# FFN input projections of a hybrid decoder trunk: Strassen's seven quarter products for eight, with the tokens on the partitions

## The chip, the cores and the metric

One core of a Trainium2 chip. The metric is the device time of one execution of the whole program, in microseconds. Activations and weights are float32 and lie in DRAM at the start; weights are laid out ahead of time by the host (copies and reorderings alone, no arithmetic).

## The reference, cut to what matters

Two layers, each a token mixer (retention in layer 0, a gated linear recurrence in layer 1) and a SwiGLU feed-forward network (FFN), each behind and ahead of an RMS norm. S = 512 tokens, D = 1024 features, FFN width 2816.

```
def rms_norm(x, g):
    y = xf * lax.rsqrt(jnp.mean(xf * xf, axis=-1, keepdims=True) + NORM_EPS)
    return y * g

def swiglu_ffn(x, w_in, w_out):
    gate, up = jnp.split(x @ w_in, 2, axis=-1)
    return (jax.nn.silu(gate) * up) @ w_out

for layer in range(2):
    m = mixer(rms_norm(x, norm_g[layer, 0]))
    x = x + rms_norm(m, norm_g[layer, 1])
    f = swiglu_ffn(rms_norm(x, norm_g[layer, 2]), ffn_w_in[layer], ffn_w_out[layer])
    x = x + rms_norm(f, norm_g[layer, 3])
```

`x @ w_in` is the FFN input projection: 512 x 1024 times 1024 x 5632.

## The kernel before

Activations are held with the features on the 128 partitions and the 512 tokens along the row. Every float32 product is made as three products of a shortened float32 format (fp32r): an operand is split into a high part (a cast) and a low part (value minus high part), and high·high, high·low and low·high are added up in PSUM (`mm3`, L189 to L191). Weights arrive as raw chunks of 128x1024, loaded by SP's queue; ACT makes the high part (L145, `wh_...`), DVE the low part (L146, `wl_...`). Four raw chunks are loaded ahead and up to eight are held split.

The order of the program is written by a recording scheme: PE's products are issued one after another, and work of the other engines is put off by so many ns of products (`Later`); each engine then works through its own list in order.

Between two matrix products stands a norm. `out_proj` ends with `finish`, which for each half of the tokens takes 1/rms of the projection (`rchain`: a matmul sums the squares, `st_...`, DVE makes the root by a short chain, a matmul broadcasts it, `rb_...` L289), and then goes through the eight feature tiles: DVE multiplies (L358), POOL adds the residual (L362), ACT makes the high part of the next operand (L308, `Xf_0h` and so on) and the squares, POOL adds these up (L326), DVE makes the low part (L312). The FFN's input projection begins on these tiles while they are still being made: `first_groups` runs the first three groups (a group is 128 gate and 128 up columns) side by side, tile by tile, for the first half of the tokens, then for the second. The other 19 groups run one after another, with all 512 tokens. 1/rms of the FFN's own input is applied to the result (`done`: DVE multiplies gate and up by the broadcast `rb_f`, L623 and L624, ACT takes silu, L626, DVE multiplies, L627, and the product is split for the output projection). The two first passes of the value projection (`pv`) have it the other way round: there tokens are the stationary operand of PE, weights the moving one.

Of the kernel before, what the change touches and what calls it, by code (L numbers as in the profile page):

```python
# [88 lines left out]
def trunk(ctx: ExitStack, tc: tile.TileContext, t: dict):  # L89
# [36 lines left out]
    def load():  # L126
        j = st["raw"]
        nm, src, cols, _ = order[j]
        raws[j] = wp.tile([P, 1024], F32, tag="raw", name=f"wr_{nm}", bufs=WRAW)
        nc.sync.dma_start(raws[j][:, :cols], src)  # L130
        st["raw"] += 1

    def load_ahead():
        while st["raw"] < min(st["split"] + WRAW, len(order)):
            load()

    def split_next():
# [4 lines left out]
        raw = raws.pop(j)
        hi = wp.tile([P, 1024], F32R, tag="whi", name=f"wh_{nm}")
        lo = wp.tile([P, 1024], F32R, tag="wlo", name=f"wl_{nm}")
        act.copy(hi[:, :cols], raw[:, :cols])  # L145
# [697 lines left out]
```

## Time and profile before

| | |
|---|---|
| time, median of 3 runs | 1411.14 us (1411.08 to 1411.99) |
| span of the profiled execution | 1409.6 us |
| PE busy | 1383.7 us (98%) |
| DVE busy | 751.4 us (53%) |
| ACT busy | 535.4 us (38%) |
| POOL busy | 115.5 us (8%) |

The span is from the first to the last instruction of the one profiled execution; the times of the runs are some 1.5 us longer. Busy time of an engine is that in which it worked on at least one instruction; a busy PE is not a PE at its peak.

### The profile page before, as it was taken

The numbers are of one execution on the slowest core, as the hardware profiler recorded it, in microseconds if no ns is written. First come the engines' busy times: TensorE is split into PE (matmuls) and PEld (weight loads), VectorE is DVE, ScalarE is ACT, GpSimd is POOL, SyncE is SP. The second block draws the span as 40 slices with busy tenths as digits, with TensorE's granted clock in tenths as the row PEclk, the third lists the DMA queues.
The fourth block names the chain that finished last, engine by engine and source line by source line (L and its number), as shares of the span: only waits on it lengthen the run. The fifth ranks groups of instructions, "written<-read, shape, count | busy, mean of one in ns | idle before, by whom it ended". The sixth has DMA issues, their size and how long they took to land.

```text
span 1409.6 us, 17882 instructions
## 1 busy us (share of the span) xinstructions
PE 1383.7 (98%) x7128; PEld 1188.4 (84%) x7128; DVE 751.4 (53%) x1234; ACT 535.4 (38%) x793; POOL 115.5 (8%) x157
## 2 busy tenths in 40 slices
PE   8999999999999999999999999999999999999996
PEld 6888888888898888888889998888998888888886
DVE  7655455457247545444321787888486444443223
ACT  4423333335234323232222537787454222222320
POOL 1000000001015000000000610001070000000002
PEclk9999999999999999999999999999999999999998
DMA  7223232223324223322342423234342332223322
GB/s 266 90 79 94 71 103 86 76 90 120 120 77 131 94 90 101 109 90 83 128 141 91 141 83 98 90 105 137 108 146 91 94 113 92 90 82 128 104 68 68
DMA packets 49172, 146.81 MB, mean 104 GB/s; under 512 B 5728, under 2 KB 14048, under 8 KB 49088
## 3 DMA queue, kind: packets, MB, share of 16 engines
q1 hardware_dynamic: 45072, 135.16, 29.7%
q0 software_dynamic: 2864, 9.46, 2.3%
q8 instruction: 56, 0.92, 0.3%
q10 hardware_dynamic: 1152, 1.05, 0.2%
q14 instruction: 28, 0.23, 0.1%
HBM read 137.25 MB, written 8.39 MB: 103 GB/s over the span
## 4 chain that ended last, share of the span: by engine, by line
PE 66%; issue 25%; POOL 4%; DVE 2%; ACT 1%; DMA 1%; SPq 0%; POOLq 0%; DVEq 0%
PE ps_fi L190 5%; PE ps_fi L189 5%; PE ps_fi L191 5%; PE ps_fo L189 3%; PE ps_fo L191 3%; PE ps_fo L190 3%; PE ps_g L189 2%; PE ps_g L190 2%; PE ps_g L191 2%; PE ps_ro L189 2%; PE ps_ro L191 2%; PE ps_ro L190 2%; PE pv L189 2%; PE pv L191 2%; PE pv L190 2%
## 5 line engine op out<-in xcount | busy, mean ns | idle before, releaser
L146 DVE TENSOR_TENSOR wl_fi<-wr_fi,wh_fi 128x1024 fp32r<-128x1024 f32 x88 | 110.5, 1260 | 11.1 <-ACT wh_fi L145 11.1
L626 ACT ACTIVATE gr<-gr 128x512 f32<-128x512 f32 x44 | 27.8, 632 | 219.7 <-DVE gr L623 219.7
L623 DVE TENSOR_TENSOR gr<-ps_fi,rb_f 128x512 f32<-128x512 f32 x44 | 30.4, 691 | 132.8 <-PE ps_fi L191 132.8
L145 ACT CAST wh_fi<-wr_fi 128x1024 fp32r<-128x1024 f32 x88 | 91.2, 1043 | 0.0
L624 DVE TENSOR_TENSOR ur<-ps_fi,rb_f 128x512 f32<-128x512 f32 x44 | 30.4, 691 | 82.9 <-PE ps_fi L191 72.5
L146 DVE TENSOR_TENSOR wl_fo<-wr_fo,wh_fo 128x1024 fp32r<-128x1024 f32 (+1 forms) x48 | 52.9, 1132 | 33.5 <-ACT wh_fo L145 33.5
L145 ACT CAST wh_fo<-wr_fo 128x1024 fp32r<-128x1024 f32 (+1 forms) x48 | 45.0, 979 | 30.1 <-DMA wr_fo<-in_w_fo 19.4
L146 DVE TENSOR_TENSOR wl_g<-wr_g,wh_g 128x1024 fp32r<-128x1024 f32 x16 | 19.5, 1222 | 35.0 <-ACT wh_g L145 34.9
L190 PE MATMUL ps_fi<-Xf_0l,wh_fi 128*128 128x512 f32 (+1 forms) x100 | 36.5, 365 | 1.5 <-DVE Xf_0l L312 1.5
L191 PE MATMUL ps_fi<-Xf_4h,wl_fi 128*128 128x512 f32 (+1 forms) x100 | 36.5, 365 | 1.1 <-DVE wl_fi L146 1.1
L189 PE MATMUL ps_fi<-Xf_7h,wh_fi 128*128 128x512 f32 (+1 forms) x100 | 36.6, 366 | 0.6 <-ACT Xf_7h L308 0.6
L189 PE MATMUL ps_fi<-Xf_4h,wh_fi 128*128 128x512 f32 (+1 forms) x100 | 36.5, 365 | 0.4 <-ACT wh_fi L145 0.4
L190 PE MATMUL ps_fi<-Xf_7l,wh_fi 128*128 128x512 f32 (+1 forms) x100 | 36.6, 366 | 0.3
L189 PE MATMUL ps_fi<-Xf_0h,wh_fi 128*128 128x512 f32 (+1 forms) x100 | 36.6, 366 | 0.2 <-ACT ylo L352 0.2
L189 PE MATMUL ps_fi<-Xf_1h,wh_fi 128*128 128x512 f32 (+1 forms) x100 | 36.7, 367 | 0.0
L189 PE MATMUL ps_fi<-Xf_3h,wh_fi 128*128 128x512 f32 (+1 forms) x100 | 36.7, 367 | 0.0
L189 PE MATMUL ps_fi<-Xf_5h,wh_fi 128*128 128x512 f32 (+1 forms) x100 | 36.5, 365 | 0.0
L189 PE MATMUL ps_fi<-Xf_6h,wh_fi 128*128 128x512 f32 (+1 forms) x100 | 36.5, 365 | 0.0
L190 PE MATMUL ps_fi<-Xf_3l,wh_fi 128*128 128x512 f32 (+1 forms) x100 | 36.5, 365 | 0.0
L190 PE MATMUL ps_fi<-Xf_6l,wh_fi 128*128 128x512 f32 (+1 forms) x100 | 36.5, 365 | 0.0
L191 PE MATMUL ps_fi<-Xf_5h,wl_fi 128*128 128x512 f32 (+1 forms) x100 | 36.4, 364 | 0.0
L191 PE MATMUL ps_fi<-Xf_3h,wl_fi 128*128 128x512 f32 (+1 forms) x100 | 36.4, 364 | 0.0
(1375 smaller groups left out, 4420.7 us busy)
## 6 DMA issues: line engine op xcount, KB each, us to landing
wr_fi<-in_w_fi SPq DMA_DIRECT2D x88, 512.0 KB, 4.1
wr_fo<-in_w_fo SPq DMA_DIRECT2D x40, 512.0 KB, 4.4
wr_g<-in_w_g SPq DMA_DIRECT2D x16, 512.0 KB, 5.4
wr_ro<-in_w_ro SPq DMA_DIRECT2D x16, 512.0 KB, 3.8
wr_v<-in_w_v SPq DMA_DIRECT2D x13, 512.0 KB, 3.8
wr_u<-in_w_li SPq DMA_DIRECT2D x12, 512.0 KB, 3.9
wr_y<-in_w_li SPq DMA_DIRECT2D x12, 512.0 KB, 3.7
wr_lo<-in_w_lo SPq DMA_DIRECT2D x12, 512.0 KB, 3.6
```

Of the source, the lines that this page charges most:

```text
L145: act.copy(hi[:, :cols], raw[:, :cols])
L146: dve.tensor_tensor(lo[:, :cols], raw[:, :cols], hi[:, :cols].bitcast(F32), op=ALU.subtract)
L189: pe.matmul(out, lhsT=lh, rhs=rh, start=first, stop=False)
L190: pe.matmul(out, lhsT=lh, rhs=rl, start=False, stop=False)
L191: pe.matmul(out, lhsT=ll, rhs=rh, start=False, stop=last)
L623: dve.tensor_tensor(gr, ps[0], pre.rb, op=ALU.mult)
L624: dve.tensor_tensor(ur, ps[1], pre.rb, op=ALU.mult)
L626: 700, lambda: act.activation(gr, gr, AF.Silu),
```

## The change

Five sixths and more of the FFN's columns (2560 of 2816 gate and as many up columns) are taken in five pairs of 512. For one pair the tokens are cut in two halves, the 1024 inner features in two (even and odd tiles of 128), and the gate and the up columns are the two halves of the columns; the product of two by two quarters is made by Strassen's scheme in Winograd's form, with seven quarter products p1 to p7 in place of eight. Their operands are the quarters themselves and four sums each: s1 to s4 of the tokens' quarters (`Corners`), t1 to t4 of the weights' quarters (`Form`), all made in float32 by DVE and then split in high and low parts as before. Each quarter product is 24 matmuls of 128x512, with tokens as the stationary and weights as the moving operand, so results have tokens on the partitions. They are added up in three pairs of PSUM banks (A, B, C), partly by running on in the same bank, partly by ACT and DVE copies; p1 is put into B by a copy. 1/rms is then a column by partitions and goes in as the scale of silu and as the scalar of a DVE operation; its broadcast falls away. The finished result is turned back by PE (`turn`: four transposes of 128x128 in fp32, one ACT copy), and split in tiles of 1024 (`halve`). The first 256 gate and up columns are made without the scheme. In the opening, the plain columns, p1 and p2 of the first pair run side by side, tile by tile, for the first token half; then the plain columns for the second half, then p6, p5, p7, p3. The last p4 stands inside the output projection.

All big buffers come from one pool of 50 slots of 4 KB, where there were two (58 of 2 KB, and 20 for weights). Residual tiles are loaded two at a time, and two memsets a block go in the recurrence.

The diff, cut to its core:

```diff
+    class Form(Item):
+        SUMS = {"t1": ("b11", "b12"), "t2": ("t1", "b22"), "t3": ("b12", "b22"), "t4": ("t2", "b21")}
+        BEFORE = {"b11": ["t1"], "t1": ["t2"], "b21": ["t4"], "b22": ["t2", "t3"], "t2": ["t4"]}
...
+        def value(self, f):
...
+                dve.tensor_tensor(q[f, e], x, y, op=ALU.add)
...
+    class Corners:
+        SUMS = (("s1", (1, 0), (1, 1), ALU.subtract), ("s2", "s1", (0, 0), ALU.subtract),
+                ("s4", (0, 1), "s2", ALU.add), ("s3", (0, 0), (1, 0), ALU.subtract))
...
+            add(*by["s1"])
+            add(*by["s2"])
+            later.seq(lambda: None, 2500, lambda: two("s2"), 2500, lambda: two("s1"), W_S, lambda: add(*by["s3"]), 2500, lambda: two("s3"),
+                      W_S, lambda: add(*by["s4"]), 2500, lambda: two("s4"))
...
+    FIRST_PAIR = ("p1", "p2", "p6", "p5", "p7", "p3")
+    LATER_PAIR = ("p1", "p4", "p5", "p2", "p6", "p3", "p7")
+    WEIGHTS = {"p1": "b11", "p2": "b21", "p3": "b22", "p4": "t4", "p5": "t1", "p6": "t2", "p7": "t3"}
...
     def ffn(layer, pre, x_src, nxt, out, mid=None):
-        X = pre.halves[0]
-        H = [None] * KF
-
-        def done(g, ps):
-            gr, ur = big(f"gr{layer}_{g}"), big(f"ur{layer}_{g}")
-            dve.tensor_tensor(gr, ps[0], pre.rb, op=ALU.mult)
-            dve.tensor_tensor(ur, ps[1], pre.rb, op=ALU.mult)
...
-        pss = first_groups([f"fi{layer}_{g}" for g in range(FIRST)], pre)
...
+        LEFT = {"p1": (0, 0), "p2": (0, 1), "p3": "s4", "p4": (1, 1), "p5": "s1", "p6": "s2", "p7": "s3"}
+
+        def product(j, r, banks, first):
+            for e in range(2):
+                with Chunk("s", layer, j, WEIGHTS[r], e) as w:
+                    for p in range(2):
+                        for i in range(2):
+                            x = pre.left(LEFT[r], 2 * e + i, p)
+                            mm3(banks[p], x, [z[:, i * S:(i + 1) * S] for z in w], first and not e + i, e + i == 2, True)
+
+        def turn(hs, put):
+            for m in range(hs[0].shape[-1] // 256):
+                ps = aux(f"turn{layer}")
+                for c in range(2):
+                    for p in range(2):
+                        pe.transpose(ps[:, c * 256 + p * P:][:, :P], hs[p][:, m * 256 + c * P:][:, :P], ident)
+                act.copy(put(m), ps.rearrange("p (m t) -> p m t", m=2))
...
+        def closed(half):
+            hs = [big(f"hr{layer}_{half}_{p}", kind="hr") for p in range(2)]
+            for p in range(2):
+                act.copy(hs[p], C[p])
...
+            elif r == "p7":
+                for p in range(2):
+                    dve.tensor_tensor(kept["p5"][p], kept["p5"][p], B[p], op=ALU.subtract)
+                kept["c22"] = kept["p5"]
+            elif r == "p3":
+                hs, g = kept["u"], kept["g0"]
+                for p in range(2):
+                    dve.tensor_tensor(hs[p], C[p], hs[p], op=ALU.subtract)
+                for p in range(2):
+                    dve.scalar_tensor_tensor(out=hs[p], in0=hs[p], scalar=pre.cols[p], in1=g[p], op0=ALU.mult, op1=ALU.mult)
+                later.after(W_TURN, lambda: turn(hs, lambda m: to[m][:, :, :256]))
+            elif r == "p4":
...
+                    act.activation(g[p], B[p], AF.Silu, scale=pre.cols[2 + p])
+                if j < PAIRS - 1:
+                    for p in range(2):
+                        act.copy(B[p], A[p])
...
+        BANK = {"p1": A, "p2": A, "p6": B, "p7": B, "p4": B, "p5": C, "p3": C}
```

How the order moves. The first place is DVE's list in the opening of layer 0, about where the broadcast of 1/rms for the second half of the tokens (`rb_postro_256`) is first used; in the kernel before, L358 is the multiplication of a tile by it, L312 an operand's low part, L146 a weight's low part:

```order
L358 TENSOR_TENSOR yro_0_2671<-yro_0_2671,rb_postro_256_3576 128x256
L312 SCALAR_TENSOR_TENSOR Xf0_5l_3561<-yro_5_2676,ng_79,Xf0_5h_3560 128x256
L358 TENSOR_TENSOR yro_1_2672<-yro_1_2672,rb_postro_256_3576 128x256
L312 SCALAR_TENSOR_TENSOR Xf0_6l_3586<-yro_6_2677,ng_79,Xf0_6h_3585 128x256
L146 TENSOR_TENSOR wl_fi0_2_4_3618<-wr_fi0_2_4_3212,wh_fi0_2_4_3617 128x1024
L358 TENSOR_TENSOR yro_2_2673<-yro_2_2673,rb_postro_256_3576 128x256
L312 SCALAR_TENSOR_TENSOR Xf0_7l_3608<-yro_7_2678,ng_79,Xf0_7h_3607 128x256
L358 TENSOR_TENSOR yro_3_2674<-yro_3_2674,rb_postro_256_3576 128x256
L312 SCALAR_TENSOR_TENSOR Xf0_0l_3412<-yro_0_2671,ng_79,Xf0_0h_3411 128x256
L146 TENSOR_TENSOR wl_fi0_3_0_3656<-wr_fi0_3_0_3242,wh_fi0_3_0_3655 128x1024
L146 TENSOR_TENSOR wl_fi0_3_4_3662<-wr_fi0_3_4_3272,wh_fi0_3_4_3661 128x1024
```

In the changed kernel at the same place (L526 is that multiplication, L461 an operand's low part, where `Xf0_01` is the quarter of token half 0 and odd feature tiles; L158 a weight's low part, L180 a sum of weight quarters):

```order
L461 SCALAR_TENSOR_TENSOR Xf0_01l_3304<-yro_4_2546,ng_76,Xf0_01h_3303 128x256
L526 TENSOR_TENSOR yro_0_2544<-yro_0_2544,rb_postro_256_3403 128x256
L180 TENSOR_TENSOR t1_0_0_1_3426<-wr_71_3123,wr_72_3125 128x1024
L158 TENSOR_TENSOR wl_s_0_0_b11_1_3424<-wr_71_3123,wh_s_0_0_b11_1_3423 128x1024
L461 SCALAR_TENSOR_TENSOR Xf0_00l_3270<-yro_6_2547,ng_76,Xf0_00h_3269 128x256
L526 TENSOR_TENSOR yro_2_2545<-yro_2_2545,rb_postro_256_3403 128x256
L461 SCALAR_TENSOR_TENSOR Xf0_01l_3304<-yro_6_2547,ng_76,Xf0_01h_3303 128x256
L526 TENSOR_TENSOR yro_2_2545<-yro_2_2545,rb_postro_256_3403 128x256
L461 SCALAR_TENSOR_TENSOR Xf0_10l_3449<-yro_0_2544,ng_76,Xf0_10h_3448 128x256
L180 TENSOR_TENSOR t2_0_0_1_3476<-t1_0_0_1_3426,wr_73_3131 128x1024
L180 TENSOR_TENSOR t4_0_0_1_3478<-t2_0_0_1_3476,wr_74_3332 128x1024
L158 TENSOR_TENSOR wl_s_0_0_b21_1_3474<-wr_74_3332,wh_s_0_0_b21_1_3473 128x1024
```

Between the tiles of the second token half there now stand three sums and two low parts of 1024 columns, where there were three low parts; the weights of p2's second half (`b21_1`) come behind t2 and t4.

The second place is PE's list at the broadcast of 1/rms in the first groups of the kernel before (`rb_pref`, among products of 128x256):

```order
L189 MATMUL ps_fi0_1_0_3436<-Xf0_2h_3467,wh_fi0_1_0_3208 128x256
L190 MATMUL ps_fi0_1_0_3436<-Xf0_2l_3468,wh_fi0_1_0_3208 128x256
L191 MATMUL ps_fi0_1_0_3436<-Xf0_2h_3467,wl_fi0_1_0_3209 128x256
L289 MATMUL rb_pref0_0_3871<-dg_pref0_0_0_3816,ones_sq_78 128x128 [waits DVE_49,PE_49]
L289 MATMUL rb_pref0_0_3871<-dg_pref0_0_1_3818,ones_sq_78 128x128 [waits DVE_49]
L189 MATMUL ps_fi0_1_0_3436<-Xf0_3h_3495,wh_fi0_1_0_3208 128x256
L190 MATMUL ps_fi0_1_0_3436<-Xf0_3l_3496,wh_fi0_1_0_3208 128x256
L191 MATMUL ps_fi0_1_0_3436<-Xf0_3h_3495,wl_fi0_1_0_3209 128x256
```

In the changed kernel PE's list has no such broadcast; among the matmuls of a product stand groups of four transposes instead, here within p7 of the first pair (`b0_0` is a bank of B, `hr0_0` the finished result of the plain columns of token half 0):

```order
L283 MATMUL b0_1_3294<-wh_s_0_0_t3_0_3744,Xf0_s3l_3754 128x512
L281 MATMUL b0_0_3293<-wh_s_0_0_t3_1_3766,Xf0_s3h_3753 128x512
L282 MATMUL b0_0_3293<-wl_s_0_0_t3_1_3767,Xf0_s3h_3753 128x512 [waits DVE_49]
L283 MATMUL b0_0_3293<-wh_s_0_0_t3_1_3766,Xf0_s3l_3754 128x512
L827 MATMUL turn0_3842<-ident_74,hr0_0_0_3588 128x128 [waits DMAHW4_49,PE_49]
L827 MATMUL turn0_3842<-ident_74,hr0_0_0_3588 128x128 x3
L281 MATMUL b0_0_3293<-wh_s_0_0_t3_1_3766,Xf0_s3h_3753 128x512
L282 MATMUL b0_0_3293<-wl_s_0_0_t3_1_3767,Xf0_s3h_3753 128x512
```

Four transposes now stand between the third and the fourth matmul of a half product, whose second matmul waits for DVE's low part of t3.

## Rows read from the trace of the kernel before

**Rows 1.** The page: span, busy time with share and instructions of each engine, and the granted clock of PE in 40 slices of the span, in tenths.

```profile
span 1409.6 us, 17882 instructions
...
PE 1383.7 (98%) x7128; PEld 1188.4 (84%) x7128; DVE 751.4 (53%) x1234; ACT 535.4 (38%) x793; POOL 115.5 (8%) x157
...
PEclk9999999999999999999999999999999999999998
```

**Rows 2.** Busy time by stretches; the columns are the stretch, its length, then busy us and instructions of PE, PE's weight load, DVE, ACT and POOL, PE's mean granted clock, the DMA share and GB/s.

```profile
416.00:432.00 16.00, 12.65 (x98) 11.66 (x96) 12.63 (x32) 8.83 (x20) 11.50 (x14) 1.00 0.30 93
432.00:448.00 16.00, 14.39 (x114) 13.83 (x115) 12.44 (x29) 7.39 (x16) 13.47 (x15) 1.00 0.54 166
...
464.00:667.00 203.00, 203.00 (x898) 168.13 (x897) 96.97 (x138) 61.79 (x79) 0.00 (x0) 1.00 0.31 97
1021.00:1037.00 16.00, 14.71 (x117) 13.91 (x115) 13.42 (x27) 10.64 (x22) 12.53 (x14) 1.00 0.44 136
...
1055.00:1275.00 220.00, 220.00 (x1026) 184.49 (x1026) 105.99 (x150) 67.75 (x87) 0.00 (x0) 1.00 0.30 94
```

**Rows 3.** The waits of PE over the whole span: what waited, for what, us in total, times, longest.

```profile
PE pv L189 <- ACT Xr_0h L308: 6.6, 1, 6.6
...
PE ps_fi L190 <- DVE Xf_0l L312: 1.5, 1, 1.5
...
PE rb_postro L289 <- DVE dg_postro L282: 1.2, 1, 1.2
```

**Rows 4.** Timeline of PE in the value projection (tokens stationary) and in the FFN input projection of layer 0 (weights stationary); columns are start and length in us, line, operation, output<-inputs, shape, count.

```profile
19.93 0.39 PE L189 MATMUL pv<-wh_v,Xr_3h 128*128 128x512 f32 x1
...
21.52 0.39 PE L190 MATMUL pv<-wl_v,Xr_5h 128*128 128x512 f32 x1
...
599.67 0.39 PE L191 MATMUL ps_fi<-Xf_4h,wl_fi 128*128 128x512 f32 x1
...
601.93 0.39 PE L189 MATMUL ps_fi<-Xf_0h,wh_fi 128*128 128x512 f32 x1
```

**Rows 5.** The same view in the first groups of layer 0, second half of the tokens.

```profile
456.03 0.28 PE L191 MATMUL ps_fi<-Xf_3h,wl_fi 128*128 128x256 f32 x1
...
458.91 0.28 PE L191 MATMUL ps_fi<-Xf_7h,wl_fi 128*128 128x256 f32 x1
```

**Rows 6.** The broadcast of 1/rms (rb_pref): all its records grouped (length ns min/median/max), and the timeline at one of them.

```profile
L289 PE MATMUL rb_pref<-dg_pref,ones_sq x16: 270/275/278, 449.1 to 1060.1; 128*128 128x128 f32 x16
...
449.15 0.61 PE L289 MATMUL rb_pref<-dg_pref,ones_sq 128*128 128x128 f32 x4
449.51 0.36 PE L189 MATMUL ps_fi<-Xf_3h,wh_fi 128*128 128x256 f32 x1
449.71 0.28 PE L190 MATMUL ps_fi<-Xf_3l,wh_fi 128*128 128x256 f32 x1
```

**Rows 7.** Timeline of DVE in the opening of layer 0 (a bracket gives the idle time ahead and what ended it), and two rows of POOL there.

```profile
419.59 1.82 DVE L146 TENSOR_TENSOR wl_fi<-wr_fi,wh_fi 128x1024 fp32r<-128x1024 f32 x1 [0.57 <-ACT wh_fi L145]
...
426.28 0.41 DVE L358 TENSOR_TENSOR yro<-yro,rb_postro 128x256 f32<-128x256 f32 x1
...
427.01 0.42 DVE L358 TENSOR_TENSOR yro<-yro,rb_postro 128x256 f32<-128x256 f32 x1
...
427.89 0.41 DVE L358 TENSOR_TENSOR yro<-yro,rb_postro 128x256 f32<-128x256 f32 x1
...
431.27 1.53 DVE L146 TENSOR_TENSOR wl_fi<-wr_fi,wh_fi 128x1024 fp32r<-128x1024 f32 x1 [1.54 <-ACT wh_fi L145]
432.72 0.41 DVE L358 TENSOR_TENSOR yro<-yro,rb_postro 128x256 f32<-128x256 f32 x1
...
445.71 0.15 DVE L272 TENSOR_SCALAR m_pref<-st_pref 128x2 f32<-128x2 f32 x1
...
448.49 0.48 DVE L282 TENSOR_SCALAR dg_pref<-ident,y_pref 128x128 f32<-128x128 f32 x2
...
438.63 0.92 POOL L362 TENSOR_TENSOR yro<-yro,xrro 128x256 f32<-128x256 f32 x1
...
440.40 0.92 POOL L362 TENSOR_TENSOR yro<-yro,xrro 128x256 f32<-128x256 f32 x1
```

**Rows 8.** Instructions of DVE and ACT from 464 to 667 us, grouped (count | busy us, mean ns of one | idle time ahead and what ended it).

```profile
L146 DVE TENSOR_TENSOR wl_fi<-wr_fi,wh_fi 128x1024 fp32r<-128x1024 f32 x34 | 41.4, 1219 | 1.8 <-ACT wh_fi L145 1.8
L623 DVE TENSOR_TENSOR gr<-ps_fi,rb_f 128x512 f32<-128x512 f32 x19 | 13.1, 691 | 62.4 <-PE ps_fi L191 62.4
...
L145 ACT CAST wh_fi<-wr_fi 128x1024 fp32r<-128x1024 f32 x33 | 34.4, 1041 | 0.0
L626 ACT ACTIVATE gr<-gr 128x512 f32<-128x512 f32 x19 | 12.0, 632 | 105.1 <-DVE gr L623 105.1
```

**Rows 9.** Timeline of PE where the FFN input projection begins and ends, in both layers, and at one wait between.

```profile
416.27 0.28 PE L189 MATMUL ps_fi<-Xf_0h,wh_fi 128*128 128x256 f32 x1
418.09 0.39 PE L190 MATMUL ps_fi<-Xf_0l,wh_fi 128*128 128x256 f32 x1 [1.54 <-DVE Xf_0l L312]
...
667.21 0.39 PE L189 MATMUL ps_fo<-Hf_0h,wh_fo 128*128 128x512 f32 x1
...
1027.50 0.28 PE L189 MATMUL ps_fi<-Xf_0h,wh_fi 128*128 128x256 f32 x1
...
1275.25 0.39 PE L189 MATMUL ps_fo<-Hf_0h,wh_fo 128*128 128x512 f32 x1
```

More of the change, by code (lines that the diff above doesn't have):

```diff
@@ new lines, in trunk, with __init__, split, between @@
+    class Form(Item):
+        SUMS = {"t1": ("b11", "b12"), "t2": ("t1", "b22"), "t3": ("b12", "b22"), "t4": ("t2", "b21")}
+        BEFORE = {"b11": ["t1"], "t1": ["t2"], "b21": ["t4"], "b22": ["t2", "t3"], "t2": ["t4"]}
+        def __init__(self, key, new, quarters):
+            super().__init__(key, [src for _, src in new], 1024, 2720)
+            self.quarters = quarters
+            for n, (q, _) in enumerate(new):
+                quarters[q, key[-1]] = self.first + n
+        def value(self, f):
+            q, e = self.quarters, self.key[-1]
+            if (f, e) in q and isinstance(q[f, e], int):
+                q[f, e] = raws.pop(q[f, e])
+            if (f, e) not in q:
+                x, y = (self.value(z) for z in self.SUMS[f])
+                q[f, e] = slot(f"{f}_{'_'.join(map(str, self.key[1:3]))}_{e}")
+                dve.tensor_tensor(q[f, e], x, y, op=ALU.add)
+            return q[f, e]
+        def split(self):
+            f, e = self.key[3:]
+            raw = self.value(f)
+            def between():
+                for g in self.BEFORE.get(f, ()):
+                    self.value(g)
+                after = order[st["split"] + 1]
+                if isinstance(after, Form):
+                    while st["raw"] < after.loads:
+                        load()
+                    after.value(after.key[3])
+            parts = self.two(raw, between)
+            self.quarters[f, e] = None
+            if f == "t3":
+                self.quarters["b12", e] = None
+            return parts
@@ L127, in load @@
         j = st["raw"]
-        nm, src, cols, _ = order[j]
-        raws[j] = wp.tile([P, 1024], F32, tag="raw", name=f"wr_{nm}", bufs=WRAW)
-        nc.sync.dma_start(raws[j][:, :cols], src)
+        src = wanted[j]
+        raws[j] = slot(f"wr_{j}")
+        nc.sync.dma_start(raws[j][:, :src.shape[-1]], src)
         st["raw"] += 1
     def load_ahead():
-        while st["raw"] < min(st["split"] + WRAW, len(order)):
+        done = order[st["split"] - 1].loads if st["split"] else 0
+        while st["raw"] < min(done + WRAW, len(wanted)):
             load()
@@ L138, in split_next @@
         j = st["split"]
-        nm, _, cols, _ = order[j]
-        if st["raw"] == j:
+        while st["raw"] < order[j].loads:
             load()
[L142 to L145, printed above, removed]
-        dve.tensor_tensor(lo[:, :cols], raw[:, :cols], hi[:, :cols].bitcast(F32), op=ALU.subtract)
-        parts[j] = hi, lo
+        parts[j] = order[j].split()
         st["split"] += 1
@@ L466, in trunk @@
     for j in range(KD):
[L467 removed]
+        sq = big(f"sq0_{j}", kind="sq")
         act.square(sq, x0[j])
```

415 lines of the change are left out of this document (319 added, 96 removed).

## The prediction

> **What bounds the kernel now.** I read the busy shares first. [rows 1] show PE busy for 1383.7 of a span of 1409.6 us, DVE for 53%, ACT for 38%; the granted clock stands in its upper level, 2.4 GHz, in all but the last slice. The reader is to see that nothing but PE can be the limit over the whole, and that an average of 53% says little about a stage. So I read the stages next: in [rows 2] the main part of either FFN input projection (464 to 667 and 1055 to 1275) has PE busy without a gap and DVE under half busy, but the openings (416 to 448, 1021 to 1037) have PE at 79% to 92% and DVE at 78% to 84%. Last the waits of PE: those of [rows 3], the longest, are of a few us, each ended by a DVE or ACT result that makes an operand. So PE's instruction count sets the time, except in the two openings, where DVE is nearly full already.
>
> The run shown has a span of 1409.6 us and the median of the times is 1411.1, so 1.5 us lie outside the span; I carry them along unchanged.
>
> **Products.** A record's end is modelled, so I price by the distance of starts. [rows 4] give ten intervals of 128x512 from 599.67 to 601.93 us, 0.227 each. Tokens become the stationary operand and weights the moving one, as in the value projection of the retention layer; its rows there, 19.93 to 21.52 for seven intervals, give 0.227 too, so the turn of the operands costs nothing. 128x256 products have 24 intervals from 456.03 to 458.91, 0.120 each [rows 5].
>
> Per layer the old projection issues 19 groups x 48 = 912 of 128x512 and 3 x 96 = 288 of 128x256: 206.7 + 34.6 = 241.3 us. The new one issues 5 pairs x 7 products x 24 = 840 and 96 for the 256 columns done plainly: 936 x 0.2267 = 212.2. That is 29.1 us less per layer, **58.2 in both**. The broadcast of 1/rms falls away: four times the 0.36 to 0.45 us from its start to the next product's full pace [rows 6], **1.8**.
>
> **Transposes, the one PE operation the trace lacks.** 88 per layer, 176 in all, each one weight load and one matmul of 128 columns, in groups of four between products. Nearest is the fp32 128x128 broadcast: four records in 0.36 us to the next start, and that start's successor 0.20 later, so about 0.11 per record with its load [rows 6]. From below: half of a 128x256, 0.06, so 10.6 us. From above: two such records each, 0.22, so 39 us. I take 0.12, just over the nearest row: **21 us**. (0.22 would mean that a transpose runs as a full fp32 product, and the order shows one record for each.)
>
> **DVE and ACT in the steady part.** Per pair DVE has 14 splits and 8 sums of 128x1024 at 1.22 us and eight operations of 128x512 at 0.69 [rows 8]: 26.8 + 5.5 = 32.4 us. PE needs 7 x 24 x 0.2267 + 16 x 0.12 = 40.0. ACT has 14 casts at 1.04 and 14 operations of about 0.63: 23.4. So neither binds; what DVE does for a pair is hidden at 81%, and if an operation of 1024 took over 1.57 us the cover would be gone and each 0.1 above would cost 2.2 us a pair. The drains sit in between: a pair of banks is written again after at least one other product, 5.4 us, and the drain ahead is two operations of 0.69. The weights' loads are as many bytes as before and the DMA share is 0.31 there [rows 2]; I cost that at nothing, as I do the paired residual loads, the memsets that go and the slots of one pool (POOL is idle there, and a load that had to wait for a slot would be late by what exceeds its lead of some two products, 10.9 us). The last product, which stands inside the output projection with other products before and behind it, is in the count above.
>
> **The openings, where DVE is the cover.** The old stretch of layer 0 runs from 416.27 to 667.21 [rows 9]: 250.9 us, of which 241.3 are products and some 2.2 the small products of the norms, so 7.4 are lost. In layer 1 it is 1027.50 to 1275.25: 247.8, 4.3 lost. Now the walk through the new order, by DVE's durations from [rows 7]: an X tile's multiply and low part take 0.88 together, an operation of 1024 takes 1.45 start to start while POOL is at work, later 1.25.
>
> DVE's order is as before up to 426.28. From there, by the order shown with the change, three pairs and a multiply end at 429.25, sum t1 at 430.7, the low part of b11_1 at 432.15: PE, which is through with the first chunks at 429.7 and the plain part of tile 4 at 431.1, waits 0.8. Five operations of X tiles, then t2, t4 and the low part of b21_1, are done at 438.8; PE gets there at 435.05: 3.75. The low part of the plain chunk r_3 ends at 442.0, PE wants it at 440.2: 1.85. The second token half cannot begin before ACT has copied the C banks out, and those copies stand behind the high part of the last X tile, which POOL (one tile in 1.77 us, [rows 7]) and DVE deliver late: copied at 449.3, wanted at 447.2: 2.1. PE's 48 products of the rest last to 460.5. Product 6 finds its operand; product 5 wants the low part of s1, behind a chain of 2.8 us for 1/rms [rows 7] and four activations: 0.5. Product 7 wants a low part of t3 and that of s3, behind the second chain, two activations, two multiplies and a sum: DVE ends them at 475.0 and 476.3, PE is there at 472.2: 3.9. With 1.5 for the first low part, a wait that stays [rows 3], and some 0.6 around the broadcast for the second half that is 15 us against 7.4: **+7.6**. What is late next is product 3, whose s4 is just in time.
>
> In layer 1 the same walk gives 1.7 (the second half's sum of squares, behind a chunk's low part), 1.7 (its broadcast), 1.4 (b21_1), 1.7 (r_3), 3.0 (the copies of C), 0.2, 3.2 (product 7) and 1.1 of small ones, 14.0 against 4.3: **+9.7**. Both together **+17.3**, bounds: with the 1.22 of the quiet rows everywhere the 25 large operations of an opening end some 5 us sooner, so +7; with the 1.82 that one took at 419.59 [rows 7] some 8 later each, so +33.
>
> **The sum**: 1411.1 - 58.2 - 1.8 + 21 + 17.3 = 1389.4, **1390 us**. The ends of the unknown costs: 1351.1 + 10.6 + 7 = 1369, and 1351.1 + 39 + 33 = 1423.
>
> **A rule that speaks against it.** The rows show the broadcast's records lasting 0.275 us each by the profile while starts follow at about 0.11 [rows 6]. The Trainium skill, "TensorE: Matmul & The Clock Gate", Part 4 (PE-mode transpose), gives about 275 ns for a 128x128 transpose within a kernel and says that access latency is most of it. Charged in full, 176 would cost 48 us, and the sum would be 1417 instead of 1390. I go by the rows, since there the latency of one record lies beside the next.
>
> **Rivals.**
> *Transposes do not overlap* (the other side). If each held PE for the record's whole 0.275 us, 176 x 0.275 = 48.4 and the time is 1390 + 27.4 = **1417**, slower. It decides from 0.24 us each on, where the gain of 21 is used up. For it: the data are the stationary operand, loaded just ahead of use. Against: the fp32 pairs of [rows 6] do just that at 0.11. No trace shown has a transpose. Chance 0.07. It is what the figure of the Trainium skill's page above comes to.
> *The openings stay hidden.* ACT or DVE gets through sooner, since the chains wait less than I let them: 1351.1 + 21 = **1372**. For it: DVE has 3 to 4 us of idle time in each 16 of the opening [rows 2]. Against: that idle time was waiting for ACT and POOL, and the sums are new. Chance 0.17.
> *DVE sets the pace throughout.* Every one of the 70 products starts late because its split or the drain of its banks comes late; 0.3 us each is 21 us, **1411**, and no gain is left. For it: DVE at 81% in order, with sums in front of the splits of the same quarter. Against: the splits are put ahead by about two products. Chance 0.14, half of it slower.
> *The products do not shorten*, because something else than PE's count sets the pace: against it, PE busy in all of 464 to 667 [rows 2]. Chance under 0.02.
>
> **Numbers.** My forecast (1380 to 1400) has 0.6. From the rivals' times 1372 and 1411 the range is **1371 to 1409**. A measurement of this kernel tells about 0.2%, 2.8 us, from no change: faster 0.85, same 0.05, slower 0.10.
>
> **What would show it.** In the new profile the stretch from the first product of the plain columns to the first of the output projection, with the 5.4 us of the last product 4 that now stands behind it added, should last 250.9 - 29.1 - 0.9 + 10.5 + 7.6 = 239 us in layer 0 and 247.8 - 29.1 - 0.9 + 10.5 + 9.7 = 238 in layer 1. Right for the transposes: four starts of a group within about 0.5 us; 1 us or more would be the rival. Right for the openings: PE waits named after DVE's low parts of b21, r, s3 and t3 and after ACT's copies of C, some 14 us per layer, and DVE busy in 430 to 475 at over 90%. Right for the steady part: products 0.2267 apart across a whole pair with no DVE wait over 1 us. The forecast fails if the waits spread past the first pair, if the granted clock leaves 1.0 after a wait of the opening (it did not after the 6.6 us at the start, [rows 1, 3]), or if the sums of 1024 cost much more than the splits.

## The result, and the profile after

The changed kernel takes **1387.76 us** (median of 4 runs, 1387.48 to 1387.93) against 1411.18 of the kernel before beside it: a ratio of 0.9829, interval 0.9815 to 0.9843, 23.4 us less. The forecast was 1390, faster, with a range of 1371 to 1409.

The head of the page, to be laid beside [rows 1]; then the starts of the FFN input projection and of the output projection behind it in both layers, beside [rows 9].

```profile
span 1385.7 us, 17307 instructions
...
PE 1347.5 (97%) x6760; PEld 1145.3 (83%) x6760; DVE 902.3 (65%) x1320; ACT 665.5 (48%) x983; POOL 120.0 (9%) x129
```

```profile
415.73 0.40 PE L281 MATMUL c<-wh_r,Xf_00h 128*128 128x512 f32 x1
...
647.79 0.48 PE L281 MATMUL ps_fo<-hh,wh_fo 128*128 128x512 f32 x1
...
1014.51 0.40 PE L281 MATMUL c<-wh_r,Xf_00h 128*128 128x512 f32 x1
...
1244.66 0.48 PE L281 MATMUL ps_fo<-hh,wh_fo 128*128 128x512 f32 x1
```

PE is still the engine that is always busy, with 36 us less to do; DVE went from 53% to 65% of a shorter span and ACT from 38% to 48%. The stretches last 232.1 and 230.2 us. With the 5.4 of the last product 4 and 0.9 for the last eight transposes, which both lie behind their ends, that is 238.4 and 236.5, where 239 and 238 were forecast.

The waits of PE, to be laid beside [rows 3] (what waited, for what, us in total, times, longest):

```profile
PE pv L281 <- ACT Xr_0h L403: 6.1, 1, 6.1
PE a L282 <- DVE wl_s_b L158: 4.4, 2, 3.0
PE c L281 <- ACT hr L871: 4.1, 2, 2.1
PE st_postlo L354 <- DVE ssq_lo L519: 3.3, 1, 3.3
PE c L282 <- DVE wl_r L158: 2.3, 2, 1.8
PE rb_postro L384 <- DVE dg_postro L377: 1.8, 1, 1.8
PE b L281 <- ACT u L923: 1.6, 2, 0.8
...
PE c L283 <- DVE Xf_00l L461: 1.2, 1, 1.2
```

The first is the wait at the kernel's start, 6.6 us before the change; the others shown stand in the two openings. `wl_s_b` is the low part of b21_1, `wl_r` that of r_3, `hr` are the copies of the C banks and `u` those of product 6, so most places are those that the prediction walked to. The opening of layer 0 and the steady part by stretches, columns as in [rows 2]:

```profile
432.00:448.00 16.00, 11.94 (x45) 8.70 (x43) 15.91 (x20) 11.47 (x25) 15.95 (x15) 0.89 0.62 222
...
480.00:640.00 160.00, 159.34 (x737) 132.27 (x737) 130.97 (x149) 94.52 (x125) 0.00 (x0) 1.00 0.32 97
```

From 480 to 640 us PE has 0.7 us of idle time in 160 while DVE is busy for 82% of it. In the opening it is the other way round: DVE 15.91 and POOL 15.95 of 16 us, PE 11.94. A granted clock of 0.89 stands there too; in the kernel before, only the last slice of the span was below 0.9 [rows 1]. It gets an experiment of its own.

One more reading, for the transposes: their records by the lengths in ns (min/median/max), and one group in the timeline.

```profile
L827 PE MATMUL turn<-ident,u x80: 270/272/273, 491.9 to 1244.6; 128*128 128x128 f32 x80
```

```profile
491.87 1.03 PE L827 MATMUL turn<-ident,u 128*128 128x128 f32 x8
492.66 0.48 PE L281 MATMUL b<-wh_s_t,Xf_11h 128*128 128x512 f32 x1
492.98 0.40 PE L282 MATMUL b<-wl_s_t,Xf_11h 128*128 128x512 f32 x1
```

A record lasts 0.272 us, but eight of them and the next product take 1.11 us from the start of the first to the start of the product after that one. Less the 0.227 of one product, that is 0.88 for eight, 0.11 each.

In a start-to-start count over 415 to 480 us (the distance between two starts on PE, less what the instructions in it need in a quiet stretch) the opening of layer 0 loses 14.0 us against 7.6 before, and that of layer 1, over 1014 to 1080, 13.2 against 4.4.

### The profile page after: what moved, and what is told of

The parts are those of the page before. It is cut to its first block, busy times and chain, and to the rows that moved or that the text cites. A ratio compares the mean times of both kernels' runs of the same rounds, so it can differ in the third digit from the quotient of the medians.

```text
span 1385.7 us, 17307 instructions
## 1 busy us (share of the span) xinstructions
PE 1347.5 (97%) x6760; PEld 1145.3 (83%) x6760; DVE 902.3 (65%) x1320; ACT 665.5 (48%) x983; POOL 120.0 (9%) x129
## 4 chain that ended last, share of the span: by engine, by line
PE 55%; POOL 2%; DVE 2%; issue 1%; ACT 1%; DMA 0%; POOLq 0%; DVEq 0%; ACTq 0%
PE ps_fo L281 6%; PE ps_fo L283 6%; PE ps_fo L282 6%; PE b L281 3%; PE b L283 3%; PE b L282 3%; PE c L281 2%; PE c L282 2%; PE c L283 2%; PE a L283 2%; PE a L282 2%; PE a L281 2%; PE ps_y L281 1%; PE ps_y L283 1%; PE ps_y L282 1%; PE ps_lo L281 1%
## 5 line engine op out<-in xcount | busy, mean ns | idle before, releaser
L281 PE MATMUL ps_fo<-hh,wh_fo 128*128 128x512 f32 (+1 forms) x440 | 153.3, 348 | 0.0
L282 PE MATMUL ps_fo<-hl,wh_fo 128*128 128x512 f32 (+1 forms) x440 | 152.7, 347 | 0.0
L283 PE MATMUL ps_fo<-hh,wl_fo 128*128 128x512 f32 (+1 forms) x440 | 152.7, 347 | 0.0
L158 DVE TENSOR_TENSOR wl_s_t<-t,wh_s_t 128x1024 fp32r<-128x1024 f32 x80 | 96.9, 1235 | 24.5 <-ACT wh_s_t L156 24.5
L158 DVE TENSOR_TENSOR wl_s_b<-wr,wh_s_b 128x1024 fp32r<-128x1024 f32 x60 | 76.0, 1266 | 29.8 <-ACT wh_s_b L156 29.8
L282 PEld LDWEIGHTS ps_fo<-hl,wh_fo 128*128 128x128 f32 x440 | 83.4, 190 | 10.3
L281 PEld LDWEIGHTS ps_fo<-hh,wh_fo 128*128 128x128 f32 x440 | 83.4, 190 | 10.2
L283 PEld LDWEIGHTS ps_fo<-hh,wl_fo 128*128 128x128 f32 x440 | 83.4, 189 | 10.2
L156 ACT CAST wh_s_t<-t 128x1024 fp32r<-128x1024 f32 x80 | 80.7, 1051 | 0.0
L156 ACT CAST wh_s_b<-wr 128x1024 fp32r<-128x1024 f32 x60 | 61.0, 1060 | 3.3 <-DVE wl_s_t L158 3.3
L158 DVE TENSOR_TENSOR wl_fo<-wr,wh_fo 128x1024 fp32r<-128x1024 f32 (+1 forms) x48 | 51.8, 1131 | 7.9 <-ACT wh_fo L156 7.9
L180 DVE TENSOR_TENSOR t<-t,wr 128x1024 f32<-128x1024 f32 x40 | 51.7, 1292 | 0.1
L180 DVE TENSOR_TENSOR t<-wr,wr 128x1024 f32<-128x1024 f32 x40 | 49.0, 1225 | 0.0
L158 DVE TENSOR_TENSOR wl_g<-wr,wh_g 128x1024 fp32r<-128x1024 f32 x16 | 19.5, 1223 | 35.5 <-ACT wh_g L156 35.3
L282 PE MATMUL a<-wl_s_b,Xf_01h 128*128 128x512 f32 x80 | 32.4, 405 | 4.4 <-DVE wl_s_b L158 4.4
```

The lines of the kernel that those rows point to most:

```text
L156: act.copy(hi[:, :c], raw[:, :c])
L158: dve.tensor_tensor(lo[:, :c], raw[:, :c], hi[:, :c].bitcast(F32), op=ALU.subtract)
L180: dve.tensor_tensor(q[f, e], x, y, op=ALU.add)
L281: pe.matmul(out, lhsT=lh, rhs=rh, start=bool(first), stop=False, skip_group_check=chained)
L282: pe.matmul(out, lhsT=lh, rhs=rl, start=False, stop=False, skip_group_check=chained)
L283: pe.matmul(out, lhsT=ll, rhs=rh, start=False, stop=bool(last), skip_group_check=chained)
```

## Experiments

The theory to be tested is the prediction's sum: PE's count sets the time in the steady part, a transpose costs 0.11 to 0.12, DVE's work is hidden until it fills a pair, and the openings lose what the operand chain of DVE, POOL and ACT is late by. The medians of the kernel before beside these runs lay at 1411.9 to 1412.3 us, up to 1 us above that of the run above, so I go by ratios where 1 us matters.

**Does PE's count set the time?** Product 7 issued twice, eight products for seven:

```
-   mm3(banks[p], x, ..., first and not e + i, e + i == 2, True)
+   for n in range(2 if r == "p7" else 1):
+       mm3(banks[p], x, ..., first and not e + i, e + i == 2 and (r != "p7" or n), True)
```

> Quarter product p7 is issued twice, so that a pair of inner halves has eight quarter products again, everything else of the change kept (the quarter outputs that p7 enters hold it twice). 24 matmuls of 128x512 more in each of 10 pairs, at 0.2267 us: if TensorE's count sets the pace everywhere outside the openings, plus 54.4 us on 1387.8, 1442 (1439 to 1444). If stalls elsewhere in a pair would hide part of an eighth product, it is less: under 1435.

Measured 1441.91 us (1439.58 to 1442.44), ratio 1.0206 (1.0192 to 1.0220): 54.2 more than the changed kernel by the medians, 53 by the ratios, for 240 more matmuls of 128x512, so 0.22 to 0.226 each. The eighth quarter product is paid in full, and with it the change is slower than the kernel before: the seventh for the eighth is the whole gain.

**What a transpose costs.** Each one twice, and none:

```
                pe.transpose(ps[:, c * 256 + p * P:][:, :P], hs[p][:, m * 256 + c * P:][:, :P], ident)
+               pe.transpose(ps[:, c * 256 + p * P:][:, :P], hs[p][:, m * 256 + c * P:][:, :P], ident)
```

> Every transpose is issued twice (the second writes the same values again), so PE has 176 more of them. If a transpose takes PE the 0.11 us that the changed kernel's groups show from start to start, the time is 1387.8 + 176 x 0.111 = 1407.3 us. If it held PE for the whole 0.27 us of a record, 1435. If the groups stood in time that PE would have waited anyway, 1388.

Measured 1407.66 us (1406.16 to 1408.75), ratio 0.9966 (0.9953 to 0.9979): 19.9 more, 0.113 for each of 176.

```
-       ps = aux(f"turn{layer}")
-       for c in range(2):
-           for p in range(2):
-               pe.transpose(...)
-       act.copy(put(m), ps.rearrange("p (m t) -> p m t", m=2))
+       for p in range(2):
+           act.copy(put(m)[:, p], hs[p][:, m * 256:m * 256 + 256])
```

> The 176 transposes of H are left out, and ScalarE copies H to its slots from SBUF as it is (so the output is that of an H in the wrong order). If the transposes cost 0.111 to 0.12 us each, as doubling them said: 1387.8 less 19.6 to 21, 1367 to 1368. If leaving them out also takes a wait for ScalarE's copies away (the 2.1 us ahead of the second group in each layer): 1363 to 1366. If it puts H's copies later, so that the wait grows: 1369 to 1372.

Measured 1366.66 us (1366.25 to 1366.87), ratio 0.9676 (0.9663 to 0.9689): 21.1 less, 0.120 each. The two runs measure the price from both sides, and without transposes the loss of the openings stayed in sum (14.4 and 13.6 us by the same count), so nothing else went with them in sum.

**When does DVE's cover end?** The low part of 5, then of 10, of the 14 splits of a pair is made twice, in all pairs behind a layer's first:

```
     parts = self.two(raw, between)
+    if self.key[2] and (f[0] == "t" or f == "b11"):   # dve5: and e == 0
+        dve.tensor_tensor(parts[1], raw, parts[0].bitcast(F32), op=ALU.subtract)
```

> In the pairs after the first, five of fourteen low parts are made twice (same values): 6.1 us more of DVE per pair, 38.5 in place of 32.4, where PE needs 40. If DVE lies beside PE with only its sum counting, no change: 1388 to 1391. If the order within a pair binds already, up to 8 x 6.1 = 49 more: over 1400.

> As dve5, but ten of fourteen: 12.2 us more per pair, 44.6 against 40.0 of PE. If DVE's sum per pair decides, it is now the limit in the eight later pairs: 8 x 4.6 = 37 more, less what lies ahead at the start of the stretch (some 5 per layer): 1415 to 1425. If there were more room than the sum says, under 1400.

With five, 1391.37 us (1390.98 to 1392.05), ratio 0.9849 (0.9834 to 0.9863), 2.8 to 3.6 more than the changed kernel, whose interval it overlaps. With ten, 1424.37 (1423.76 to 1425.47), ratio 1.0083 (1.0068 to 1.0098): 36.6 more. By the sum a pair's DVE work is then 32.4 + 10 x 1.22 = 44.6 us against PE's 40.0, and eight pairs at 4.6 are 36.8. The stretches, of five and then of ten, and the longest waits with ten:

```profile
480.00:640.00 160.00, 157.80 (x729) 130.74 (x728) 152.02 (x167) 92.74 (x124) 0.00 (x0) 1.00 0.30 95
```

```profile
480.00:660.00 180.00, 169.54 (x760) 137.38 (x760) 177.95 (x189) 98.12 (x128) 0.00 (x0) 0.99 0.29 90
```

```profile
PE turn L829 <- DVE u L939: 10.1, 20, 1.5
PE turn L829 <- DVE h L950: 8.9, 16, 0.9
```

At 95% DVE is nearly all cover, PE losing some 2 us in 160; at 99% it is the bound, and PE's waits now stand in every pair, ahead of the transposes of what DVE drains. So the third rival (DVE sets the pace) is a true limit of this kernel, some 23% of DVE's work away by the sum (32.4 us a pair against 40.0), and some 3 us are lost ahead of it.

**Are the openings DVE's?** The eight weight sums of each layer's first pair are left out:

```
             x, y = (self.value(z) for z in self.SUMS[f])
+            if not self.key[2]:
+                q[f, e] = x
+                return x
```

> The eight weight sums t1 to t4 of the first pair of each layer are left out (the product takes the first term in place of the sum, so these columns are not the reference's): 16 DVE operations of 128x1024 fewer, none of PE's. If DVE is what is late in the opening, PE's waits for b21 (3.0 and 1.4 us), the slow matmuls behind the 3.0 us wait (1.2 us) and part of the waits for the plain chunk and for ACT's copies of C go: 1376 to 1380 us. If PE waits there for ACT, POOL or the loads, and DVE is only named because it comes last, 1386 to 1388.

Measured 1379.70 us (1376.65 to 1379.88), ratio 0.9764 (0.9749 to 0.9778): 8 to 9 less. The trace is that of the fastest run, 1376.65; in it the openings lose 10.2 and 7.6 instead of 14.0 and 13.2, 9.4 less together. Its waits:

```profile
PE c L284 <- ACT hr L874: 2.5, 2, 2.1
PE st_postlo L357 <- DVE ssq_lo L522: 2.0, 1, 2.0
```

So the sums' work is about a third of all that the openings lose (9.4 of 27.2 us), and over half of the 15.2 that the change added to them. What stays is not the sums'.

**Can the same work be put elsewhere?** Four versions moved work in the opening without leaving any out. `t4late` makes the sums t2 and t4 of the first pair each at its own split instead of ahead of b21's low part (in layer 0 for the second inner half alone):

```
-    for g in self.BEFORE.get(f, ()):
+    late = not self.key[2] and (self.key[1] or e)
+    for g in self.BEFORE.get(f, ()) if not late or f not in ("b21", "t2") else ():
...
```

> Of the first pair, t2 is made when t2 is split and t4 not before t4 is split (in layer 0 for the second inner half alone, whose sums fall into the opening); the rest is as changed. The waits for b21 lose two sums each. If each wait is a cost of its own, 3.0 + 1.2 + 1.4 and part of the 3.3 of layer 1 go: 1380 us. If the opening is one chain, in which ACT's copies of C stand behind the last tile and that behind all of DVE's work, those copies come only one sum (1.45 us) sooner per layer and take the waits over: 1384 to 1386.

Measured 1389.53 us (1389.14 to 1390.57), ratio 0.9836 (0.9822 to 0.9851): no gain. Its waits say where part of it went, and two rows of layer 1 (a wait, then a stretch) where the rest did:

```profile
PE c L285 <- ACT hr L875: 6.1, 2, 4.5
...
PE st_postlo L358 <- DVE ssq_lo L523: 2.0, 1, 2.0
```

```profile
1047.68 0.80 PE L285 MATMUL c<-wh_r,Xf_10h 128*128 128x512 f32 x1 [4.51 <-ACT hr L875]
```

```profile
1048.00:1052.00 4.00, 4.00 (x10) 3.13 (x10) 3.42 (x6) 2.40 (x6) 0.00 (x0) 0.50 0.00 0
```

The 4.4 us for b21's low parts are nearly gone (1.2), those for the copies of C grew from 4.1 to 6.1. Expected were 1380 if each wait had its own cost and 1384 to 1386 if part of it moved on; the run missed both. The waits are not all of it: in layer 1 the second token half began 0.7 us sooner than in the changed kernel (1047.68 against 1048.36), but behind this wait the granted clock was 0.50, as it was not behind the 2.06 us there before, and the next sum of squares for 1/rms started 1.65 us later (1053.58 against 1051.93). So the loss moved on, in part to a longer wait and in part to a lower clock behind it; what `t4late` would gain with PE kept busy in that wait was not tried.

`step18` spaces the X tiles of the second token half 1800 ns apart in the order of the program, instead of 1200, so that ACT's copies of C stand ahead of the last tiles; `late_step18` does that and makes the sums t2 and t4 later as well; `v_1400_600` is `t4late` with 1400 ns, the operand s2 split sooner and the first copies of C recorded 100 planned ns sooner. The edit of `step18`:

```
-    later.after(STEP if pre is not None else 0, lambda: add(j + 1))
+    later.after(0 if pre is None else 1800 if a and isinstance(pre, Corners) else STEP, lambda: add(j + 1))
```

> In the second token half of the opening the feature tiles follow each other 1800 planned ns apart in place of 1200; nothing is added or left out. ACT's copies of C then stand ahead of the last two tiles. If those copies are late because of their place in ACT's list, both waits of 2.1 us go: 1383.5 us. If the last tile or s2 is then late for the second half's products, the wait only moves: 1387 to 1390.

> As step18, and the sums t2 and t4 of the first pair are made when t2 is split, not when b21 is, so they stand behind the weights that PE wants first. If the order of DVE's work is what costs, the waits for b21 (3.0 and 1.4), the 1.2 of slow matmuls and most of those for the copies of C go: 1378 to 1381 us. If DVE's whole work up to product 5 or 7 is what costs, the waits come back at products 6, 5 or 7 and the time is 1385 to 1388.

> As t4late; besides, the tiles of the second token half follow each other 1400 planned ns apart instead of 1200 and the split of s2 is recorded 600 ns behind its sum instead of 2500, so ACT's copies of C stand ahead of the last tile and the cast of s2 ahead of the silus that wait for 1/rms. One chain through the copies of C: the waits of 2.1 go as well, 1378 to 1381 us. If s2 is the next thing late, 1384 to 1388.

Measured 1405.70 us (1404.60 to 1406.20), ratio 0.9952 (0.9937 to 0.9967); 1408.18 (1407.00 to 1411.66), ratio 0.9968 (0.9955 to 0.9980); 1391.86 (1391.26 to 1393.31), ratio 0.9853 (0.9836 to 0.9869). All three missed what either theory expected. The waits of `step18`, then two rows of its ACT:

```profile
PE b L281 <- ACT Xf_s2h L477: 12.7, 2, 6.8
...
PE c L283 <- DVE Xf_s4l L478: 3.8, 2, 1.9
```

```profile
458.98 1.33 ACT L915 ACTIVATE g<-g,y_pref 128x512 f32<-128x512 f32 x2 [4.83 <-DVE y_pref L371]
...
464.11 1.04 ACT L477 CAST Xf_s2h<-Xf_s 128x1024 fp32r<-128x1024 f32 x1 [2.60 <-DVE Xf_s L473]
```

The wait for the copies did fall away, but product 6's operand s2 now hangs on the SiLUs. In layer 0 ACT's list has them at 458.98, where they waited 4.83 us for 1/rms; behind them stands ACT's copy of the last tile (461.02), from which DVE makes s1 and s2 (to 464.0), and only then comes the high part of s2 (464.11). PE stands still for 6.8 and 5.9 us. That was not in either expectation: I had followed the copies, and not what the later tiles push behind another chain on the same in-order engine. In `v_1400_600` this wait is gone, and those for the copies of C (4.4) and of product 6 (4.0) took its place.

**What does POOL do to the opening?** The adds of squares of the second token half are left out on POOL:

```
-    eng.tensor_tensor(self.ssq[:, a:b], self.ssq[:, a:b], sq[:, a:b], op=ALU.add)
+    if not a or not isinstance(self, Corners):
+        eng.tensor_tensor(self.ssq[:, a:b], self.ssq[:, a:b], sq[:, a:b], op=ALU.add)
```

> POOL's seven adds of squares of the second token half are left out in each layer (1/rms of that half is then that of its first tile, and the output is not the reference's); POOL keeps its residual adds. Between 434.9 and 449.3 us POOL had no idle time in layer 0, and ScalarE's copies of C stand behind activations that wait for POOL's residual adds. If POOL's pace is what makes the copies late: the two waits of 2.06 us for them go, those for b21's and r_3's low parts shrink with DVE's operations (1.75 down towards 1.25 us): 1387.8 less 4 to 8, 1380 to 1384. If DVE's order of work sets the opening and POOL only lies beside it: less than 1.5 us gained, 1386.3 to 1388.

The rows of the changed kernel that led to it, of POOL, of DVE and of ACT:

```profile
440.75 0.92 POOL L421 TENSOR_TENSOR pssq_f<-pssq_f,psq_f 128x256 f32<-128x256 f32 x1
441.64 1.71 POOL L530 TENSOR_TENSOR yro<-yro,xrro 128x256 f32<-128x256 f32 x1
443.31 1.72 POOL L421 TENSOR_TENSOR pssq_f<-pssq_f,psq_f 128x256 f32<-128x256 f32 x1
```

```profile
441.00 1.75 DVE L158 TENSOR_TENSOR wl_r<-wr,wh_r 128x1024 fp32r<-128x1024 f32 x1
442.68 1.75 DVE L158 TENSOR_TENSOR wl_s_t<-t,wh_s_t 128x1024 fp32r<-128x1024 f32 x1
```

```profile
447.70 0.51 ACT L455 ACTIVATE Xf_11h<-yro,ng 128x256 fp32r<-128x256 f32 x1 [0.54 <-POOL yro L530]
...
449.77 1.04 ACT L871 COPY hr<-c 128x512 f32<-128x512 f32 x2
```

Measured 1384.63 us (1381.49 to 1384.82), ratio 0.9799 (0.9783 to 0.9816): 3.1 less, 4 by the ratios: 0.6 us short of what the POOL theory expected (1380 to 1384) and out of the other's range. In its trace the copies and a low part read so:

```profile
PE a L282 <- DVE wl_s_b L158: 3.3, 2, 2.5
...
PE c L281 <- ACT hr L872: 1.4, 2, 0.7
```

```profile
442.23 1.21 DVE L158 TENSOR_TENSOR wl_s_t<-t,wh_s_t 128x1024 fp32r<-128x1024 f32 x1
```

The wait for the copies fell from 4.1 to 1.4 us, and this operation, `wl_s_t`, from 1.75 to 1.21. So POOL is part of the chain in two ways, by the tiles that it delivers late and by what it costs DVE. It is not all of it: the waits for the low parts and for the sum of squares stayed.

**Does the lower clock cost anything?** Behind the 3.0 us wait the changed kernel's products come 0.43 us apart, and the granted clock is 0.50 (1.2 GHz), in both layers; behind waits of 2.06 us in the same trace it was 1.00. The timeline of PE, then two stretches:

```profile
439.38 0.80 PE L282 MATMUL a<-wl_s_b,Xf_01h 128*128 128x512 f32 x1 [3.02 <-DVE wl_s_b L158]
...
440.40 0.63 PE L281 MATMUL a<-wh_s_b,Xf_01h 128*128 128x512 f32 x1
440.83 0.63 PE L282 MATMUL a<-wl_s_b,Xf_01h 128*128 128x512 f32 x1
...
442.81 0.50 PE L282 MATMUL c<-wl_r,Xf_00h 128*128 128x512 f32 x1 [0.50 <-DVE wl_r L158]
```

```profile
440.00:442.00 2.00, 2.00 (x6) 1.30 (x4) 2.00 (x4) 2.00 (x5) 2.00 (x3) 0.50 0.59 216
1024.00:1026.00 2.00, 2.00 (x6) 1.57 (x5) 1.69 (x13) 0.25 (x1) 0.00 (x0) 0.50 0.95 354
```

`fill` puts ten products that nobody reads into each of the two waits:

```
+    def fill(n):
+        ps = aux("fill")
+        for _ in range(n):
+            pe.matmul(ps[:, :P], lhsT=ident, rhs=ones_sq, start=True, stop=True)
     ...
+            if name == "postlo" and a:
+                fill(10)
     ...
+                            if not layer and e == 2 and i:
+                                fill(10)
```

> Ten 128x128 matmuls whose result nobody reads (about 2.2 us of TensorE together) go ahead of the first quarter product with b21_1 in layer 0 (a 3.0 us wait in the changed kernel) and ahead of the second st_postlo in layer 1 (a 3.3 us wait). They lie in the wait and take nothing of its work away. If the clock falls behind those two waits because TensorE stands still in them, the rows behind them are 0.227 us apart instead of 0.43 and 3.2 us less is lost: 1384.5 to 1385. If it falls for another reason, or the extra work costs as much as it saves: 1387.5 to 1388.5.

Measured 1387.78 us (1387.50 to 1387.94), ratio 0.9826 (0.9812 to 0.9839): no change at all. Its rows at the same places:

```profile
439.37 0.50 PE L282 MATMUL a<-wl_s_b,Xf_01h 128*128 128x512 f32 x1 [1.60 <-DVE wl_s_b L158]
...
440.17 0.40 PE L282 MATMUL a<-wl_s_b,Xf_01h 128*128 128x512 f32 x1
440.41 0.39 PE L283 MATMUL a<-wh_s_b,Xf_01l 128*128 128x512 f32 x1
...
442.80 0.50 PE L282 MATMUL c<-wl_r,Xf_00h 128*128 128x512 f32 x1 [1.77 <-DVE wl_r L158]
```

```profile
440.00:442.00 2.00, 1.03 (x5) 0.50 (x3) 2.00 (x4) 2.00 (x5) 2.00 (x3) 1.00 0.61 226
1024.00:1026.00 2.00, 1.48 (x7) 0.89 (x5) 1.69 (x13) 0.22 (x1) 0.00 (x0) 1.00 0.99 360
```

The clock stayed at 1.00 in both places and the products came 0.23 apart, so it had fallen there because PE stood still. And nothing was won. In layer 0 the operand `wl_r` came at 442.80 instead of 442.81, and PE waited 1.77 us for it instead of 0.50. In layer 1 the broadcast `rb_postlo` waited 1.3 us for its operand, where it had waited for nothing, and started 0.2 us sooner than before. The expectation had the mechanism right and left out the next wait.

One more place of `fill` is in none of this, the product behind the copies of C in layer 1:

```profile
1048.28 0.50 PE L281 MATMUL c<-wh_r,Xf_10h 128*128 128x512 f32 x1 [2.03 <-ACT hr L880]
```

```profile
1050.00:1052.00 2.00, 2.00 (x6) 1.51 (x6) 1.97 (x3) 0.48 (x1) 0.00 (x0) 0.50 0.01 4
```

There the clock fell behind a wait of 2.03 us, where the changed kernel had kept 1.00 behind 2.06, so the length of a wait does not tell by itself. PE was 1.5 us later by the next sum of squares (1053.42 against 1051.93), and the wait of 0.8 us at product 7 was gone; at the end of the stretch 0.2 us of it were left (1244.88 against 1244.66). `noturn` shows the like in layer 0: its clock was at 0.50 from 440 to 444 and products came 0.43 apart until 447.7, yet the wait of 2.06 us for the copies is gone, and the product behind them starts at 450.27 instead of 450.38.

## Why the prediction was right, point by point

- **Products, -58.2.** Right: an added matmul cost 0.22 to 0.226 where 0.2267 stood in the sum, and seven quarter products instead of eight paid in full. The 1.8 for the broadcast that falls away was measured by no run.
- **Transposes, +21 at 0.12.** Right, measured from both sides at 0.113 and 0.120. The rival at 0.275 each (1417) fell: records are 0.272 us long, and starts 0.11 apart. The figure of about 275 ns in the Trainium skill, "TensorE: Matmul & The Clock Gate", Part 4 (PE-mode transpose), is about the length of such a record in this trace (270 to 273 ns), and its cost among other products here is under half of it.
- **The steady part, at nothing.** Right: PE 159.34 of 160 us, DVE 82% where 81% was worked out. The cost past the cover's end was that of the sum: 36.6 us measured, 36.8 worked out, with DVE's work at 44.6 us per pair. At 38.5 us, where the sum gives nothing, some 3 were lost.
- **The openings, +17.3.** Measured 6.4 + 8.8 = 15.2, so the term was 2 us too large, and with it the sum: 1411.2 - 58.2 - 1.8 + 20.5 + 15.2 = 1386.9, against 1387.8 measured. Inside it most places were right and single sizes were not:

| wait, us | forecast | measured |
|---|---|---|
| layer 0: first low part of X | 1.5 | 1.2 |
| its broadcast | 0.6 | 1.8 |
| b11_1 | 0.8 | 0 |
| b21_1 (its high part 0.5 too) | 3.75 | 3.5 |
| r_3 | 1.85 | 0.5 |
| copies of C | 2.1 | 2.1 |
| products 5 and 7 | 4.4 | 0.8 |
| layer 1: sum of squares, broadcast | 3.4 | 3.3 |
| b21, r_3 | 3.1 | 3.2 |
| copies of C | 3.0 | 2.1 |
| products 5 and 7 | 3.4 | 0.8 |

  The step that failed is the walk past the second chain for 1/rms: product 7 was to wait 3.9 and 3.2 us for the low parts of t3 and s3, and it waited 0.8 in each layer, for ACT's copies of product 6. In layer 0 these low parts ended at 473.7 and 474.9, where 475.0 and 476.3 were forecast, and PE was there at 473.3 and not at 472.2. DVE was not as full there as I had it: 39.26 us of the 45 from 430 to 475 (87%), where over 90% was to be seen.

  The waits of this table come to 19.3 us, where the walk had 29.0 (with 1.1 of small ones). The rest of the count, 7.9 us, is what the walk had no term for: the slower spacing behind two waits and some 0.15 to 0.2 us at each restart. The slower spacing stands where waits were forecast for r_3 in layer 0 (1.85) and for the broadcast in layer 1 (1.7); in `fill`, without it, these waits measured 1.77 and 1.3. So it is in part luck that the term came out within 2 us: too much, chiefly at product 7, and too little at the restarts nearly cancelled. The upper bound of the term has a slip as well: 25 operations at 1.82 instead of 1.45 are 9.3 us and not some 8, so that end of the sum is 1426 and not 1423.
- **"The forecast fails if the granted clock leaves 1.0."** It did leave it, and the forecast held. I had taken the clock for a cost by itself; `fill` shows that the time lay ahead of a wait that ends at nearly the same instant anyway. The reading given with it, that the clock did not leave 1.0 after the 6.6 us at the start, was of the clock's column alone. The starts say otherwise, in the kernel before (7.21, 7.64, 8.07) as in the changed one:

```profile
7.17 0.63 PE L283 MATMUL pv<-wh,Xr_0h 128*128 128x512 f32 x1
7.59 0.63 PE L281 MATMUL pv<-wh,Xr_1h 128*128 128x512 f32 x1
```

  They are 0.43 us apart, as in the stretches at 0.50, until 12.2 us (12.3 before), while the column shows 1.00.
- **The rival "openings stay hidden" (1372).** It fell. Without the sums' work (`nosum0`, 1379.7) the openings still lost 17.8 us, where the kernel before lost 12.0.
- **Left open.** Which single operation holds the openings. The runs show that sums, POOL's adds and the order on ACT each hold a part, and that moving one brings the wait, or a lower clock, back elsewhere. Taking the adds of squares off POOL in a way that keeps their result was not tried, and no version that still computes the reference beat the changed kernel.

## What to carry to other kernels

Seven products for eight pay what PE's count says only as long as the engine that makes the sums keeps a margin: add up its work per pair from quiet rows, and what is lost past that margin can be worked out beforehand (36.8 us here, 36.6 measured). In an opening where several in-order engines hand operands to each other, look at the chain and not at the single wait: in the four versions here that only moved work nothing was gained, and in the two that left work of the opening out, something was. Before a slow stretch is priced, look at what ends the next wait; here some 2.6 us ahead of two such waits cost nothing.

## What the runs showed of the hardware

- The granted clock fell to 0.50 behind waits of 3.0 and 3.3 us in the middle of work, and ten products whose result is thrown away, put into each of these waits, kept it at 1.00 there. It had not fallen behind the waits of 2.06 us in the same trace, but in `fill` it did behind one of 2.03.
- Behind the first wait of the kernel (6.15 us) matmuls of 128x512 start 0.43 us apart until 12.2 us, the spacing of the 0.50 stretches, while the column of the granted clock shows 1.00: the spacing of starts tells more there than the column.
- In the rows above a POOL add of 128x256 takes 0.92 us or 1.71 to 1.72. The long ones start while DVE is in an operation of 128x1024 on two operands in SBUF, the short one at 440.75 started ahead of `wl_r`; `wl_s_t` takes 1.75 there and 1.21 in `noadd`, where no add runs beside it. The Trainium skill, "SBUF — State Buffer", section "SBUF: two separate sides", says that GpSimd and a VectorE operation with two SBUF inputs lock a shared pair of ports for a whole instruction; these rows agree.
